# Instance norm on one core: 32 units of 4 MB in six slots, or 23 units of 4 and 6 MB in four slots

## The chip, the core and the metric

The kernel runs on one core of a Trainium2 chip. TensorE (PE in the profile), VectorE (DVE), ScalarE (ACT), GpSimd (POOL) and SyncE (SP) each follow their own instruction stream; 16 DMA engines move data between HBM, the chip's main memory, and SBUF, the on-chip memory of 128 partitions. The metric is the device time of one execution in microseconds (us), lower is better.

## The reference

```python
x: (4, 8, 16, 256, 256) float32          # 512 channels of 65536 places
gamma: (8, 16) float32                   # one factor for each of 128 channels
mu = x.mean(axis=(3, 4), keepdims=True)
var = ((x - mu) ** 2).mean(axis=(3, 4), keepdims=True)
out = (x - mu) / np.sqrt(var + 1e-5) * gamma[None, :, :, None, None]
```

Each channel is 256 KB. x is 134.2 MB and so is the output; x does not fit in SBUF, and every channel is read once and written once.

## The kernel before, in words

The flat array is cut into 32 units of 4 MB, 16 channels each. In SBUF a unit has 128 partitions with 8192 float32 (32 KB) in each, so that 8 partitions hold one channel. Six tiles `xt0` to `xt5` of 32 KB a partition are the slots; unit u lives in slot u % 6 (lines 45 to 48). Nothing is scheduled by a planner: each engine runs its instructions in the order in which the program writes them.

At the start, six loads are issued, units 1 and 3 on ACT's DMA queue and the others on SP's (lines 56 and 57). POOL issues two small transfers, a write of 16 times 512 B into the output (`touch`, line 54) and the read of gamma (line 55), and then makes `navg` (lines 63 to 72), a 128 x 128 matrix that holds -1/65536 wherever two partitions belong to one channel. DVE and PE spread gamma into `g_col`, one column for each of the eight possible positions of a unit (lines 80 to 91).

Then follows one loop over the units (line 104). For each unit:

- DVE sums each partition (line 106), ACT sums the squares (line 107);
- PE multiplies both sums with `navg` (line 115), which gives every partition minus its channel's mean and minus its mean square;
- DVE makes minus the variance (116), ACT its root (120), DVE the reciprocal (124) and the product with gamma (126);
- DVE normalises in place, (x - mu) * scale, one instruction over all 8192 columns (135). In unit 0 alone DVE takes 5120 columns and ACT the other 3072 (132);
- ACT's queue issues the store (139), and SP's queue issues the load of unit u + 6 (141). That load waits until the store of unit u has ended, since they share a slot.

Loads and stores thus stand in two queues, SP's and ACT's, which feed the same 16 DMA engines. Each transfer gives each engine eight rows, one row for each partition.

The program's lines follow.

Of the kernel before, what the change touches and what calls it, by code (L numbers as in the profile page):

```python
# [1 line left out]

# [4 lines left out]

F32 = mybir.dt.float32
U8 = mybir.dt.uint8
ALU = mybir.AluOpType  # L10
ACTF = mybir.ActivationFunctionType
AX = mybir.AxisListType


@with_exitstack
def kernel(
    ctx: ExitStack,
    tc: tile.TileContext,
    x: bass.AP,
    gamma: bass.AP,  # L20
    out: bass.AP,
):
    nc = tc.nc
    B, G, C, H, W = x.shape
    P = nc.NUM_PARTITIONS
    HW = H * W
    n_ch = B * G * C
    S = 8
    K = P // S
    F = HW // S  # L30
    U = n_ch // K
    NG = (G * C) // K
    AHEAD = 6
    assert HW % S == 0 and (G * C) % K == 0

    xv = x.rearrange("b g c h w -> (b g c h w)").rearrange("(u p f) -> u p f", p=P, f=F)
    ov = out.rearrange("b g c h w -> (b g c h w)").rearrange("(u p f) -> u p f", p=P, f=F)
# [9 lines left out]
    def load(u, queue):  # L47
        queue.dma_start(out=slots[u % AHEAD][:], in_=xv[u])  # L48


    g_row = singles.tile([1, G * C], F32, name="g_row")
    touch = singles.tile([16, 128], F32, name="touch")
    nc.vector.memset(touch[:], 0.0)  # L53
    nc.gpsimd.dma_start(out=ov[0][0::S, 0:128], in_=touch[:])  # L54
# [6 lines left out]
    one = singles.tile([1, 1], F32, name="one")  # L61
    nc.gpsimd.memset(one[:], 1.0)
    navg = singles.tile([P, K, S], F32, name="navg")
    nc.gpsimd.memset(navg[:], -1.0 / HW)  # L64
    nc.gpsimd.affine_select(  # L65
        out=navg[:], in_=navg[:], pattern=[[-S, K], [0, S]], compare_op=ALU.is_ge,
        fill=0.0, base=0, channel_multiplier=1,
    )
    nc.gpsimd.affine_select(  # L69
        out=navg[:], in_=navg[:], pattern=[[S, K], [0, S]], compare_op=ALU.is_ge,  # L70
        fill=0.0, base=S - 1, channel_multiplier=-1,
    )
    navg_w = navg[:].rearrange("p k s -> p (k s)")
    root_eps = singles.tile([P, 1], F32, name="root_eps")
    nc.scalar.activation(out=root_eps[:], in_=eps_t[:], func=ACTF.Sqrt)  # L75
    g_rep = singles.tile([1, NG, K, S], F32, name="g_rep")
    g_ps = psum.tile([P, NG], F32, name="g_ps", bufs=1)
    g_col = singles.tile([P, NG], F32, name="g_col")

    nc.vector.tensor_copy(  # L80
        out=g_rep[:],
        in_=g_row[:].rearrange("o (n k) -> o n k", n=NG).unsqueeze(3).to_broadcast([1, NG, K, S]),
    )
    for n in range(NG):
        nc.tensor.matmul(  # L85
            out=g_ps[:, n : n + 1],
            lhsT=g_rep[:, n].rearrange("o k s -> o (k s)"),
            rhs=one[:],
            start=True, stop=True,
        )  # L90
    nc.vector.tensor_copy(out=g_col[:], in_=g_ps[:])  # L91

    junk = singles.tile([P, F], U8, name="junk")

    st = singles.tile([P, U, 2], F32, name="st")
# [5 lines left out]
    shift = singles.tile([P, 1], F32, name="shift")  # L101

    squares = []
    for u in range(U):
        t = slots[u % AHEAD]
        nc.vector.reduce_sum(out=st[:, u, 0:1], in_=t[:], axis=AX.X)  # L106
        square = nc.scalar.activation(  # L107
            out=junk[:], in_=t[:], func=ACTF.Square, accum_out=st[:, u, 1:2],
        )
        if u:  # L110

            tc.declare_no_dep(square.ins, squares[-1].ins, reason="junk, ordered by the root between")
        squares.append(square)
        ps = psum.tile([P, 2], F32, name="ps")
        nc.tensor.matmul(out=ps[:], lhsT=navg_w, rhs=st[:, u], start=True, stop=True)  # L115
        nc.vector.tensor_scalar(  # L116
            out=nvar[:, u : u + 1], in0=ps[:, 0:1], scalar1=ps[:, 0:1],
            scalar2=ps[:, 1:2], op0=ALU.mult, op1=ALU.add,
        )
        nc.scalar.activation(  # L120
            out=std[:, u : u + 1], in_=nvar[:, u : u + 1], func=ACTF.Sqrt,
            bias=eps_t[:], scale=-1.0,
        )
        nc.vector.reciprocal(out=rstd[:, u : u + 1], in_=std[:, u : u + 1])  # L124
        g = u % NG
        nc.vector.tensor_mul(  # L126
            out=scale[:, u : u + 1], in0=rstd[:, u : u + 1], in1=g_col[:, g : g + 1],
        )
        cut = F * 5 // 8 if u == 0 else F
        if cut < F:  # L130
            nc.vector.tensor_mul(out=shift[:], in0=ps[:, 0:1], in1=scale[:, u : u + 1])  # L131
            nc.scalar.activation(  # L132
                out=t[:, cut:], in_=t[:, cut:], func=ACTF.Identity, bias=shift[:], scale=scale[:, u : u + 1],
            )
        nc.vector.tensor_scalar(  # L135
            out=t[:, :cut], in0=t[:, :cut], scalar1=ps[:, 0:1], scalar2=scale[:, u : u + 1],
            op0=ALU.add, op1=ALU.mult,
        )
# [6 lines left out]
_INS = ['x', 'gamma']  # L145
_OUTS = [((4, 8, 16, 256, 256), 'float32')]


# [23 lines left out]
```

## Time and profile before

| | |
|---|---|
| three runs | 626.85, 626.98, 627.24 us; median 626.98 |
| profiled execution | span 625.2 us; the profile has no other time for it, and the median lies 1.7 us above the span |
| bytes moved | 268.46 MB, a mean of 429 GB/s over the span |
| busy share of the span | DVE 71%, ACT 39%, PE 3%, POOL 0% |
| DMA engines | 9 tenths or more of every 40th of the span but the first and last, which show 8 |
| rows of 32 KB on the two queues | 4352 on ACT's (q10: 32 stores and 2 loads), 3840 on SP's (q1: 30 loads) |
| first unit landed, last unit landed | 22.8 us, 585.5 us |
| last store issued | 600.6 us |

In the profile, an engine's busy time counts only its computing instructions. DMA queues are numbered; q1 is the one that SP feeds and q10 the one that ACT feeds, q0 is POOL's. A transfer of the kernel appears in them as 128 data packets and 16 packets of 4 B, one for each DMA engine, which report its end. The profile's line numbers are those of the program above.

### The profile page before, as it was taken

How to read it: one execution, taken by the hardware profiler on the slowest of the kernel's cores; microseconds unless marked ns; L12 is line 12 of the kernel's file. 1: busy time of each engine (PE TensorE's matmuls, PEld its weight loads, DVE VectorE, ACT ScalarE, POOL GpSimd, SP SyncE). 2: the span in 40 equal slices, each digit the busy share in tenths (PEclk: the TensorE clock that was granted, in tenths of full speed). 3: DMA queues.
4: the chain of work that ended last, by engine and by line, in shares of the span. 5: the costliest groups of instructions: out<-in, count | busy, mean ns of one | idle time of the engine just before them, and what ended most of it. 6: DMA issues, size and time to landing. Idle time of an engine off the chain costs nothing.

```text
span 625.2 us, 635 instructions
## 1 busy us (share of the span) xinstructions
PE 21.4 (3%) x80; PEld 19.5 (3%) x80; DVE 441.8 (71%) x164; ACT 241.8 (39%) x99; POOL 2.4 (0%) x11
## 2 busy tenths in 40 slices
PE   0200000000000000000000000000000000000000
PEld 0200000000000000000000000000000000000000
DVE  0589999998776687666786767867668676687730
ACT  0464444444443244432344423444224442244400
POOL 1000000000000000000000000000000000000000
DMA  8999999999999999999999999999999999999998
GB/s 370 436 407 432 436 436 436 436 436 430 423 436 434 434 428 434 434 436 436 436 436 428 426 436 436 432 430 434 434 436 436 436 436 421 432 436 434 434 430 367
DMA packets 9282, 268.46 MB, mean 429 GB/s; under 512 B 1072, under 2 KB 1088, under 8 KB 1088
## 3 DMA queue, kind: packets, MB, share of 16 engines
q10 hardware_dynamic: 4896, 142.61, 52.9%
q1 hardware_dynamic: 4320, 125.83, 46.8%
q0 software_dynamic: 64, 0.01, 0.0%
q14 instruction: 2, 0.02, 0.0%
HBM read 134.22 MB, written 134.23 MB: 429 GB/s over the span
## 4 chain that ended last, share of the span: by engine, by line
another core or an unknown queue 61%; DMA 17%; DVE 15%; SPq 1%; PE 1%; issue 0%; ACT 0%
DMA xt<-in_x_dram 10%; DVE st L106 10%; DMA out_dram<-xt 8%; DVE xt L135 5%; SPq L48 1%; PE ps L115 1%; ACT std L120 0%; DVE nvar L116 0%; DVE rstd L124 0%; DVE scale L126 0%; DVE shift L131 0%
## 5 line engine op out<-in xcount | busy, mean ns | idle before, releaser
L106 DVE TENSOR_REDUCE st<-xt 128x1 f32<-128x8192 f32 x32 | 277.9, 8684 | 102.2 <-DMA xt<-in_x_dram 102.2
L107 ACT ACTIVATE junk<-xt 128x8192 uint8<-128x8192 f32 x32 | 225.0, 7030 | 272.0 <-DMA xt<-in_x_dram 233.8
L135 DVE TENSOR_SCALAR xt<-xt,ps,scale 128x8192 f32<-128x8192 f32 (+1 forms) x32 | 144.0, 4500 | 1.1
L120 ACT ACTIVATE std<-nvar,eps_t 128x1 f32<-128x1 f32 x32 | 9.4, 295 | 79.4 <-DVE nvar L116 79.4
L115 PE MATMUL ps<-st,navg 128*128 128x2 f32 x64 | 17.8, 348 | 557.3 <-DVE st L106 557.3
L115 PEld LDWEIGHTS ps<-st,navg 128*128 128x128 f32 x64 | 16.0, 310 | 559.1 <-issue 546.2
L116 DVE TENSOR_SCALAR nvar<-ps 128x1 f32<-128x1 f32 x32 | 9.2, 286 | 23.8 <-PE ps L115 23.8
L124 DVE RECIPROCAL rstd<-std 128x1 f32<-128x1 f32 x32 | 5.2, 163 | 11.6 <-ACT std L120 11.6
L80 DVE COPY g_rep<-g_row 1x1024 f32<-1x1024 f32 x1 | 0.7, 681 | 14.4 <-DMA g_row<-in_gamma_dram 14.4
L107 ACT ACTIVATION_READ_ACCUMULATOR junk<-xt 128x1 f32 x32 | 6.0, 186 | 0.0
L126 DVE TENSOR_TENSOR scale<-rstd,g_col 128x1 f32<-128x1 f32 x32 | 5.1, 158 | 1.1
L85 PE MATMUL g_ps<-one,g_rep 1*128 1x1 f32 x16 | 3.5, 347 | 16.3 <-DVE g_rep L80 16.3
L85 PEld LDWEIGHTS g_ps<-one,g_rep 1*128 1x128 f32 x16 | 3.5, 326 | 16.3 <-issue 16.3
L132 ACT ACTIVATE xt<-xt,shift,scale 128x3072 f32<-128x3072 f32 x1 | 2.9, 2947 | 0.7 <-DVE shift L131 0.7
L91 DVE COPY g_col<-g_ps 128x8 f32<-128x8 f32 x1 | 0.2, 167 | 3.7 <-PE g_ps L85 3.7
L75 ACT ACT_TABLE_LOAD x1 | 1.3, 1283 | 1.7 <-PEq L156 1.7
L53 DVE MEMSET touch<- 16x128 f32 x1 | 0.2, 165 | 0.9 <-PEq L156 0.9
L54 POOL DMA_DIRECT2D out_dram<-touch x1 | 0.6, 617 | 0.8 <-DVE touch L53 0.8
L55 POOL DMA_DIRECT2D g_row<-in_gamma_dram x1 | 0.5, 487 | 0.0
L65 POOL TENSOR_SCALAR_AFFINE_SELECT navg<-navg 128x128 f32<-128x128 f32 x1 | 0.4, 400 | 0.1
L69 POOL TENSOR_SCALAR_AFFINE_SELECT navg<-navg 128x128 f32<-128x128 f32 x1 | 0.4, 399 | 0.1
L64 POOL MEMSET navg<- 128x128 f32 x1 | 0.2, 230 | 0.0
(8 smaller groups left out, 1.0 us busy)
## 6 DMA issues: line engine op xcount, KB each, us to landing
out_dram<-xt ACTq DMA_DIRECT2D x32, 4096.0 KB, 62.5
xt<-in_x_dram SPq DMA_DIRECT2D x30, 4096.0 KB, 38.5
xt<-in_x_dram ACTq DMA_DIRECT2D x2, 4096.0 KB, 31.7
out_dram<-touch POOLq DMA_DIRECT2D x1, 8.0 KB, 9.3
g_row<-in_gamma_dram POOLq DMA_DIRECT2D x1, 0.5 KB, 13.5
```

Source lines behind the costliest of these rows:

```text
L48: queue.dma_start(out=slots[u % AHEAD][:], in_=xv[u])
L75: nc.scalar.activation(out=root_eps[:], in_=eps_t[:], func=ACTF.Sqrt)
L85: nc.tensor.matmul(out=g_ps[:, n : n + 1], lhsT=g_rep[:, n].rearrange("o k s -> o (k s)"), rhs=one[:], start=True, stop=True,)
L106: nc.vector.reduce_sum(out=st[:, u, 0:1], in_=t[:], axis=AX.X)
L107: square = nc.scalar.activation(out=junk[:], in_=t[:], func=ACTF.Square, accum_out=st[:, u, 1:2],)
L115: nc.tensor.matmul(out=ps[:], lhsT=navg_w, rhs=st[:, u], start=True, stop=True)
L116: nc.vector.tensor_scalar(out=nvar[:, u : u + 1], in0=ps[:, 0:1], scalar1=ps[:, 0:1], scalar2=ps[:, 1:2], op0=ALU.mult, op1=ALU.add,)
L120: nc.scalar.activation(out=std[:, u : u + 1], in_=nvar[:, u : u + 1], func=ACTF.Sqrt, bias=eps_t[:], scale=-1.0,)
L124: nc.vector.reciprocal(out=rstd[:, u : u + 1], in_=std[:, u : u + 1])
L126: nc.vector.tensor_mul(out=scale[:, u : u + 1], in0=rstd[:, u : u + 1], in1=g_col[:, g : g + 1],)
L132: nc.scalar.activation(out=t[:, cut:], in_=t[:, cut:], func=ACTF.Identity, bias=shift[:], scale=scale[:, u : u + 1],)
L135: nc.vector.tensor_scalar(out=t[:, :cut], in0=t[:, :cut], scalar1=ps[:, 0:1], scalar2=scale[:, u : u + 1], op0=ALU.add, op1=ALU.mult,)
```

## The change

Units now have 4 or 6 MB: two of 4, thirteen of 6, two of 4, five of 6 and one of 4, 23 in all. There are four slots of 48 KB a partition (the SBUF that the slots take stays at 192 KB a partition). A row of a 6 MB unit is 48 KB in a partition, which is three thirds of 4096 columns. A channel is 16 such thirds, so it starts in the first, second or third third of a partition, and a unit has 24 channels.

All loads are issued on SP's queue. The last unit is split between DVE and ACT in the normalising step as unit 0 is.

For a 6 MB unit the sums are made for each third (one DVE instruction with three results, three ACT instructions). Three PE products add them up into means on 72 partitions, where partition j * 24 + k stands for channel k as seen from third j (`navg3`). The variance, root, reciprocal and gamma are computed on these 72; `coef` puts minus the mean and the scale into column j of each; a fourth product with `back` brings them to the 128 partitions, one column a third (`wide`, in PSUM). DVE then normalises third by third, three instructions. Units of 4 MB go the old way. New helper matrices are made on POOL and DVE ahead of the loop, and gamma is spread in another way.

The core of the diff:

```diff
-    S = 8
-    K = P // S
-    F = HW // S
-    AHEAD = 6
+    F = 4096
+    SLOTS = 4
+    K = 24
+    sizes = [2] * 2 + [3] * 13 + [2] * 2 + [3] * 5 + [2]
+    U = len(sizes)
+    starts = [sum(sizes[:i]) for i in range(U)]
+    helped = (0, U - 1)
+    def rows(flat, u):
+        lo = starts[u] * P * F
+        return flat[lo : lo + sizes[u] * P * F].rearrange("(p f) -> p f", p=P)
-    psum = ctx.enter_context(tc.tile_pool(name="psum", bufs=4, space=bass.MemoryType.PSUM))
+    psum = ctx.enter_context(tc.tile_pool(name="psum", bufs=2, space=bass.MemoryType.PSUM))
-    slots = [data.tile([P, F], F32, name=f"xt{i}") for i in range(AHEAD)]
+    slots = [data.tile([P, 3 * F], F32, name=f"xt{i}") for i in range(SLOTS)]
+    def home(u):
+        return slots[u % SLOTS][:, : sizes[u] * F]
+    def load(u):
+        nc.sync.dma_start(out=home(u), in_=rows(xf, u))
-    for u in range(AHEAD):
-        load(u, nc.scalar if u in (1, 3) else nc.sync)
+    for u in range(SLOTS):
+        load(u)
...
+    navg2 = band("navg2", [P, 16, 8], -1.0 / HW, 0, 1, [[-8, 16], [0, 8]], 7)
+    in16 = band("in16", [P, 16], 1.0, 0, 1, [[-8, 16]], 7)
+    navg3 = band("navg3", [P, 3, 3, K], -1.0 / HW, 0, 3, [[1, 3], [0, 3], [-16, K]], 15)
+    mine = band("mine", [3 * K, 3], 1.0, 0, 1, [[-K, 3]], K - 1)
+    place = singles.tile([3 * K, 3, P], F32, name="place")
...
+    nc.vector.reduce_sum(out=back[:], in_=place[:].rearrange("q j p -> q p j"), axis=AX.X)
...
     for u in range(U):
+        t = home(u)
+        three = sizes[u] == 3
+        n = sizes[u] if three else 1
+        step = sizes[u] * F // n
+        nc.vector.reduce_sum(
+            out=st[:, u, :n, 0], in_=t.rearrange("p (j f) -> p j f", j=n), axis=AX.X,
+        )
+        for j in range(n):
+            square = nc.scalar.activation(
+                out=junk[:, :step], in_=t[:, j * step : (j + 1) * step],
+                func=ACTF.Square, accum_out=st[:, u, j, 1:2],
+            )
...
+        for j in range(n):
+            nc.tensor.matmul(
+                out=ps[:q],
+                lhsT=navg3[:, j].rearrange("p j k -> p (j k)") if three else navg2[:].rearrange("p k s -> p (k s)"),
+                rhs=st[:, u, j], start=j == 0, stop=j == n - 1,
+            )
...
+        if three:
+            nc.vector.tensor_scalar_mul(out=coef[:, u, 0], in0=mine[:], scalar1=ps[:q, 0:1])
...
+            nc.vector.tensor_scalar(
+                out=coef[:, u, 1], in0=mine[:], scalar1=rstd[:q, u : u + 1],
+                scalar2=g_ch[:, m : m + 1], op0=ALU.mult, op1=ALU.mult,
+            )
+            wide = psum.tile([P, 2, 3], F32, name="wide")
+            nc.tensor.matmul(
+                out=wide[:].rearrange("p v j -> p (v j)"), lhsT=back[:],
+                rhs=coef[:, u].rearrange("p v j -> p (v j)"), start=True, stop=True,
+            )
+            for j in range(3):
+                nc.vector.tensor_scalar(
+                    out=t[:, j * F : (j + 1) * F], in0=t[:, j * F : (j + 1) * F],
+                    scalar1=wide[:, 0, j : j + 1], scalar2=wide[:, 1, j : j + 1],
+                    op0=ALU.add, op1=ALU.mult,
+                )
...
-        nc.scalar.dma_start(out=ov[u], in_=t[:])
-        if u + AHEAD < U:
-            load(u + AHEAD, nc.sync)
+        nc.scalar.dma_start(out=rows(of, u), in_=t)
+        if u + SLOTS < U:
+            load(u + SLOTS)
```

More of the change, by code (lines that the diff above doesn't have):

```diff
@@ L43 @@
     ctx.enter_context(tc.manual_schedule())
-    slots = [data.tile([P, F], F32, name=f"xt{i}") for i in range(AHEAD)]
-    def load(u, queue):
-        queue.dma_start(out=slots[u % AHEAD][:], in_=xv[u])
-    g_row = singles.tile([1, G * C], F32, name="g_row")
+    slots = [data.tile([P, 3 * F], F32, name=f"xt{i}") for i in range(SLOTS)]
[3 more added lines that the diff above has]
+        nc.sync.dma_start(out=home(u), in_=rows(xf, u))
+    g_row = singles.tile([1, GC], F32, name="g_row")
@@ L62, with band @@
-    nc.gpsimd.memset(one[:], 1.0)
-    navg = singles.tile([P, K, S], F32, name="navg")
-    nc.gpsimd.memset(navg[:], -1.0 / HW)
-    nc.gpsimd.affine_select(
-        out=navg[:], in_=navg[:], pattern=[[-S, K], [0, S]], compare_op=ALU.is_ge,
+    ones = singles.tile([1, P], F32, name="ones")
+    nc.gpsimd.memset(ones[:], 1.0)
+    def band(name, shape, value, base, multiplier, pattern, top):
+        w = singles.tile(shape, F32, name=name)
+        nc.gpsimd.memset(w[:], value)
+        nc.gpsimd.affine_select(
+            out=w[:], in_=w[:], pattern=pattern, compare_op=ALU.is_ge,
+            fill=0.0, base=base, channel_multiplier=multiplier,
+        )
+        nc.gpsimd.affine_select(
+            out=w[:], in_=w[:], pattern=[[-a, n] for a, n in pattern], compare_op=ALU.is_ge,
+            fill=0.0, base=top - base, channel_multiplier=-multiplier,
+        )
+        return w
@@ new lines @@
+    nc.gpsimd.affine_select(
+        out=place[:], in_=place[:], pattern=[[-385, 3], [-3, P]], compare_op=ALU.is_ge,
+        fill=0.0, base=15, channel_multiplier=16,
+    )
+    root_eps = singles.tile([P, 1], F32, name="root_eps")
+    nc.scalar.activation(out=root_eps[:], in_=eps_t[:], func=ACTF.Sqrt)
+    nc.vector.reduce_sum(out=back[:], in_=place[:].rearrange("q j p -> q p j"), axis=AX.X)
+    eighth = singles.tile([3 * K, 9, 8], F32, name="eighth")
+    nc.gpsimd.memset(eighth[:], 1.0)
@@ L76 @@
[L76 to L89, printed above, removed]
-        )
@@ new lines @@
+    sixteens = sorted({8 * starts[u] % GC for u in range(U) if sizes[u] == 2})
+    g_some = singles.tile([P, 16], F32, name="g_some")
+    g_col = singles.tile([P, len(sixteens)], F32, name="g_col")
+    for n, c in enumerate(sixteens):
+        nc.vector.tensor_mul(out=g_some[:], in0=g_all[:, c : c + 16], in1=in16[:])
+        nc.vector.reduce_sum(out=g_col[:, n : n + 1], in_=g_some[:], axis=AX.X)
+    junk = singles.tile([P, 2 * F], U8, name="junk")
+    st = singles.tile([P, U, 3, 2], F32, name="st")
@@ L99 @@
     scale = singles.tile([P, U], F32, name="scale")
-    shift = singles.tile([P, 1], F32, name="shift")
+    shift = singles.tile([P, U], F32, name="shift")
+    coef = singles.tile([3 * K, U, 2, 3], F32, name="coef")
     squares = []
     for u in range(U):
[L105 to L108, printed above, removed]
-        )
-        if u:
-            tc.declare_no_dep(square.ins, squares[-1].ins, reason="junk, ordered by the root between")
-        squares.append(square)
-        ps = psum.tile([P, 2], F32, name="ps")
-        nc.tensor.matmul(out=ps[:], lhsT=navg_w, rhs=st[:, u], start=True, stop=True)
+        t = home(u)
[4 more added lines that the diff above has]
+            out=st[:, u, :n, 0], in_=t.rearrange("p (j f) -> p j f", j=n), axis=AX.X,
+        )
+        for j in range(n):
[3 more added lines that the diff above has]
+            )
+            if squares and j == 0:
+                tc.declare_no_dep(square.ins, squares[-1].ins, reason="junk, ordered by the root between")
+            squares.append(square)
+        q = 3 * K if three else P
+        ps = psum.tile([P, 2], F32, name="ps")
+        for j in range(n):
[4 more added lines that the diff above has]
+            )
```

100 lines of the change are left out of this document (65 added, 35 removed).

## The prediction

> **What bounds the kernel now.** I read the DMA part of the page first, since the page's chain of waits names mostly transfers, then cut the span into stretches, then looked at what the engines wait for.
>
> The queues, from the page (packets, MB, share of the 16 engines' time in the span):
>
> ```profile
> q10 hardware_dynamic: 4896, 142.61, 52.9%
> q1 hardware_dynamic: 4320, 125.83, 46.8%
> ```
>
> The two queues together take 99.7% of the DMA engines' time. The stretches say the same (columns: length, busy time of PE, PE's weight loads, DVE, ACT and POOL, the granted clock, DMA share, GB/s); the four are the loads alone, the first store's start, the long middle, and a part of the tail in which only stores are left:
>
> ```profile
> 2.00:31.00 29.00, 3.54 (x16) 3.48 (x16) 9.07 (x3) 8.34 (x4) 1.55 (x6) 1.00 0.99 425
> 31.00:47.00 16.00, 1.11 (x4) 1.00 (x4) 13.65 (x11) 10.66 (x5) 0.00 (x0) 1.00 0.99 406
> 47.00:585.00 538.00, 16.15 (x58) 14.50 (x58) 405.02 (x146) 215.10 (x87) 0.00 (x0) 1.00 1.00 433
> 600.00:620.00 20.00, 0.00 (x0) 0.00 (x0) 0.58 (x1) 0.00 (x0) 0.00 (x0) 1.00 1.02 439
> ```
>
> The DMA share is 1.00 for 538 us. In the trace's packet records nearly every 32 KB row takes 1213 ns and starts 1209 ns after the one before it on its DMA engine, for loads and stores, in the first slices of the middle as in the last, with both queues alive as with one. 16 x 32768 B / 1209 ns is 433.7 GB/s, the middle's 433. So the DMA engines bound the kernel, from their first packet at 1.8 us to their last at 623.9 us. SP's waits and the groups show the other side:
>
> ```profile
> SPq L48 <- DMA out_dram<-xt: 514.7, 26, 39.7
> ```
>
> ```profile
> L106 DVE TENSOR_REDUCE st<-xt 128x1 f32<-128x8192 f32 x32 | 277.9, 8684 | 102.2 <-DMA xt<-in_x_dram 102.2
> L107 ACT ACTIVATE junk<-xt 128x8192 uint8<-128x8192 f32 x32 | 225.0, 7030 | 272.0 <-DMA xt<-in_x_dram 233.8
> L135 DVE TENSOR_SCALAR xt<-xt,ps,scale 128x8192 f32<-128x8192 f32 (+1 forms) x32 | 144.0, 4500 | 1.1
> ```
>
> Loads wait 514.7 us for slots, and DVE, the busiest engine, still waits 102.2 us for loads. Neither wait costs anything as long as a row of some transfer stands ready for every DMA engine. The change is therefore worth what it does to the DMA engines' work, less any moment in which it leaves both queues empty.
>
> **The DMA work.** Each transfer gives each engine eight rows and one packet of 4 B.
>
> - Before: 64 transfers, 512 rows of 32 KB an engine: 512 x 1.209 = 619.0 us; 64 packets of 4 B, 6 ns each from start to start: 0.4. Sum 619.4.
> - A 48 KB row is not in the trace. The records have 512 B rows 23.3 ns from start to start, so the slope up to 32 KB is (1209 - 23.3) / (32768 - 512) = 0.03676 ns a byte and a row's fixed part is 23.3 - 18.8 = 4.5 ns. A 48 KB row is then 1209 + 16384 x 0.03676 = 1811.3 ns. From both sides: without any saving 1.5 x 1209 = 1813.5; cut into three pieces of 16 KB, 3 x (4.5 + 602.3) = 1820.3. I take 1811.3, since 1213 ns holds for 8192 rows without a sign of a further limit.
> - After: 46 transfers. The 5 units of 4 MB give 80 rows an engine, 96.7 us; the 18 of 6 MB give 288 rows, 521.65; 46 x 6 ns is 0.3. Sum 618.65.
>
> Difference: **-0.74 us**. The ends: the first packet starts at 1.8 us, and the 1.3 us behind the last packet stay. The remaining 2.7 us between first and last packet are start-up losses: the engines start up to 1.0 us apart, the first row takes 0.4 to 0.75 us more, and around 41.5 us, as the first store starts, each engine loses 0.3 to 1.2 us (mean about 0.85; it makes the 406 GB/s above). I keep them: after starts one load and one first store too. Bounds: the store's loss gone, -0.85; twice, +0.85.
>
> **Does a queue always have work?** What one 6 MB unit takes, from the rows:
>
> - Sum of a partition, L106: 8684 ns for 8192 columns, so 13.0 us for 12288.
> - Squares on ACT run beside it. L132's 3072 columns take 2.95 us and 8192 take 7.03, so 4096 take 3.8; three, with three reads of the sum at 0.19, 11.9 us. Hidden under 13.0; otherwise the excess would be added.
> - From the end of L106 to the start of L135 the trace has 1.8 us. Two more products (0.56 each), the fourth with its hand-over (0.75) and one more small DVE step (0.2) make 3.8.
> - Normalising: 5120 columns take 2.94, 8192 take 4.55, so 4096 take 2.4; three, 7.2. Both scalars now come from PSUM; before, one did, so I leave the price; bounds are 2.4 and, at L106's rate of 1.06 ns a column, 4.3 each.
>
> DVE needs 24.0 us a unit (29.7 at the worst bound). The DMA engines need 2 x 8 x 1.811 = 29.0. Round a slot: load 29.0 beside a store at equal shares, DVE 24.0, store 29.0, and about 4 for issue, first packet and report twice; 86 of 4 x 29.0 = 116 us. 30 us of the turn are waiting in queues.
>
> I followed the rows of one DMA engine through both queues, alternating while both have work. The same walk on the kernel before gives the last landing at 581 and the last row at 621.4, against 585.5 and 623.9 measured; the start-up losses make up the latter. After:
>
> - Start: the first loads alone fill SP's queue until 1.8 + 0.7 + 16 x 1.209 + 16 x 1.811 = 50.8 us. Unit 0 lands at 13, not at 22.8. DVE first finishes the new set-up. POOL's matrices have some 820 columns against 128 (each pass 0.23 to 0.40 us for 128): until about 10 us; gamma at 15.5 at the latest, as before; then some twenty small DVE steps of 0.16 to 0.4. Unit 0 starts between 14 and 20, and its store is issued at 28 to 34. Cover: 17 us; every us past that costs one.
> - Middle: the load of unit u + 4 is issued about 12 us before the load ahead of it ends, and a unit is ready about 20 us before its store's turn.
> - Tail: the last unit lands about 35 us before the end. It needs 8.7 + 1.8 + 3.0 + 1.6 = 15 us to its store, and ahead of it are 24 us of other stores. Unit 21 is ready 10 us before its turn. Cover 9 us.
>
> So nothing shows. The moved loads: units 1 and 3 leave ACT's queue for SP's; ACT saves two issues (0.4 us each), which bound nothing, and SP issues them in 0.33 each while the first rows run. The semaphore waits in the changed program's order name, for every load, the store of its slot and transfers that ended long before; no instruction waits ahead of a shorter one.
>
> Sum against the profiled execution: 625.2 - 0.74 = 624.5; with the 1.75 us by which the median lies above the span, **626.2 us**. That is -0.12%, inside the 0.2% (1.25 us) that a measurement of this kernel can tell from no change.
>
> **The rivals.**
>
> - *The store's start loses nothing* because no loads stand ahead of it in ACT's queue: 626.2 - 0.85 = 625.4. For it: in before the loss falls where ACT's queue goes from loads to stores. Against: it strikes SP's row at 41.5 hardest, which is a load.
> - *A fixed cost a transfer on a lone queue.* Hidden while the other queue has rows, bare where one is alone. After has two such boundaries at the start (SP alone until 30 us). Nearest row: 0.85 for a queue that starts; 2 x 0.85 = +1.7, 627.9. Against: the stores alone run at 439 GB/s across two boundaries. The Trainium skill's page "DMA: Bandwidth & Descriptors", section "Anatomy of one DMA — SWDGE (gpsimd) path", fits a transfer as 2.0 us plus bytes at 436 GB/s; exposed everywhere, that would make 18 fewer transfers worth 36 us, an estimate that the 433 GB/s of the middle refute, and at two boundaries alone 4 us.
> - *Rows are not moved whole.* In 16 KB pieces: 288 x 9.0 ns = +2.6, 628.8, slower. For it: no row above 32 KB is in the trace.
> - *DVE becomes the bound*: slower. It decides at 29.0 us of DVE a 6 MB unit; at 30.3 the 18 units wait 18 x 1.3 = 23 us, about 650. For it: the PSUM bound reaches 29.7, so 0.7 x 18 = 13, about 639. Against: L135 reads ps from PSUM already and keeps its rate.
>
> **How the numbers follow.** Forecast 0.49 (own range 625.8 to 627.0), store's start 0.25, lone queue 0.06, pieces 0.10, DVE 0.07, unnamed and slower 0.03. Faster by over 0.2% is the second, 0.25, with 0.01 from the forecast's edge; slower are pieces, DVE and the rest, 0.20; the rest 0.54. The range takes in all but DVE and the unnamed: 625.2 to 628.9.
>
> **What would show it.** Each of q1 and q10 with 23 x 144 = 3312 packets (pieces: above 7500); the stretch from 60 to 580 us at share 1.00 and 434 GB/s; rows of 48 KB at about 1815 ns; first store near 30 us with a dip of GB/s beside it; DVE near 24 us a unit and waiting for loads in every one. Wrong: a slice under 9 tenths in the middle or ahead of the last store, or DVE not waiting.

## The result, and the profile after

| | before | after |
|---|---|---|
| median | 626.94 us (626.78 to 627.28, 8 runs) | 628.17 us (627.15 to 629.76, 8 runs) |
| profiled execution | span 625.2 us | 627.41 us, span 625.7 us |

The ratio is 1.0022, 95% interval 1.0012 to 1.0032: slower by 1.2 us, where 0.7 us less was forecast. The runs of after also lie 2.6 us apart, those of before 0.5. (Ratios leave out single executions far above the others of their kernel, so for kernels whose runs scatter the ratio is smaller than that of the medians.) The profiled run of after, 627.41 us, is the second shortest of its eight.

The queues and the instruction fetches, from the page of after (packets, MB, share):

```profile
q1 hardware_dynamic: 3312, 134.22, 49.9%
q10 hardware_dynamic: 3312, 134.22, 49.6%
q14 instruction: 4, 0.03, 0.0%
q8 instruction: 1, 0.02, 0.0%
```

3312 is 23 x 144 for each queue: every 48 KB row is one packet. The records give it 1815 ns, and 1812 from start to start, where 1811.3 was forecast. The last two lines are engines that load their own instructions, by one packet for each block, called a fetch here; in before q14 has two packets. The prediction did not look at these lines.

Stretches of after, in the columns that the prediction names (`...` stands for lines not shown):

```profile
31.00:47.00 16.00, 0.56 (x2) 0.50 (x2) 14.82 (x6) 8.70 (x4) 0.00 (x0) 1.00 1.00 407
...
66.00:585.00 519.00, 25.26 (x140) 23.02 (x140) 378.43 (x145) 209.00 (x125) 0.00 (x0) 1.00 1.00 434
...
600.00:620.00 20.00, 0.56 (x2) 0.50 (x2) 3.66 (x6) 3.24 (x2) 0.00 (x0) 1.00 0.99 427
620.00:622.00 2.00, 0.00 (x0) 0.00 (x0) 0.00 (x0) 0.00 (x0) 0.00 (x0) 1.00 1.02 442
622.00:624.00 2.00, 0.00 (x0) 0.00 (x0) 0.00 (x0) 0.00 (x0) 0.00 (x0) 1.00 0.27 115
```

The same end in before:

```profile
620.00:622.00 2.00, 0.00 (x0) 0.00 (x0) 0.00 (x0) 0.00 (x0) 0.00 (x0) 1.00 0.83 360
622.00:624.00 2.00, 0.00 (x0) 0.00 (x0) 0.00 (x0) 0.00 (x0) 0.00 (x0) 1.00 0.42 180
```

The middle is as forecast, 434 GB/s at share 1.00. The news is in the end, from 622 to 624 us. A share of 0.42 or 0.27 does not say whether all engines stop together or a few go on; the packet records, below, do. The waits of SP's queue and the groups:

```profile
SPq L61 <- DMA out_dram<-xt: 537.8, 19, 45.8
```

```profile
L173 DVE TENSOR_REDUCE st<-xt 128x3 f32<-128x12288 f32 (+1 forms) x23 | 276.6, 12025 | 104.8 <-DMA xt<-in_x_dram 104.8
L177 ACT ACTIVATE junk<-xt 128x4096 uint8<-128x4096 f32 (+1 forms) x59 | 230.4, 3906 | 282.7 <-DMA xt<-in_x_dram 267.0
L215 DVE TENSOR_SCALAR xt<-xt,wide 128x4096 f32<-128x4096 f32 x54 | 127.6, 2420 | 13.3 <-PE wide L210 13.3
```

DVE waits 104.8 us for loads and loads wait 537.8 us for slots: no engine became the bound.

**The last DMA engine decides.** Each transfer gives each of the 16 DMA engines eight rows, even to one that is 17.9 us behind the others (sp_late5, below). The 4 B packet with which each engine closes the last store tells when it was done. In the profiled executions (us; the run's own time beside it):

```
kernel        median engine   last three            run
before           623.4        623.5 623.5 623.9     (span 625.2)
after            622.7        623.8 624.1 624.2     627.41
after2           624.6        625.5 626.3 627.7     630.89
lean             622.3        623.1 623.3 627.7     630.89
pad              623.5        623.6 624.7 627.8     630.79
padsplit         623.3        623.5 625.5 625.5     628.55
join             623.2        623.6 623.7 624.0     627.12
sp               623.5        624.0 625.6 627.0     630.31
actloads         622.7        624.2 624.8 626.1     629.20
after_late4      622.5        626.3 626.8 627.2     630.31
after_late6      622.4        623.3 623.7 626.7     629.84
sp_late5         665.5        665.6 665.6 668.5     671.75
```

In every line that has the run's time, this is 3.0 to 3.3 us above its last engine's end. The median engine of after ends 0.8 us before that of before, 622.7 against 623.4, close to the forecast -0.74. The mean of the sixteen falls by 0.27 us only, from 623.33 to 623.06, and the last engine ends 0.24 us later; in after2, the same kernel again, it ends 3.8 us later. So the rows shrank as forecast, and what single engines lose ate it.

### The profile page after: what moved, and what is told of

Read it like the earlier page. It is cut to its first block, busy times and chain, and to the rows that moved or that the text cites. A ratio compares the mean times of both kernels' runs of the same rounds, so it can differ in the third digit from the quotient of the medians.

```text
span 625.7 us, 854 instructions
## 1 busy us (share of the span) xinstructions
PE 29.1 (5%) x156; PEld 26.3 (4%) x156; DVE 446.7 (71%) x193; ACT 250.1 (40%) x145; POOL 6.3 (1%) x25
## 3 DMA queue, kind: packets, MB, share of 16 engines
q1 hardware_dynamic: 3312, 134.22, 49.9%
q10 hardware_dynamic: 3312, 134.22, 49.6%
## 4 chain that ended last, share of the span: by engine, by line
DMA 41%; another core or an unknown queue 37%; DVE 16%; PE 1%; ACT 1%; issue 1%; SPq 0%; POOL 0%; ACTq 0%
DMA out_dram<-xt 22%; DMA xt<-in_x_dram 17%; DVE st L173 10%; DVE xt L215 3%; DMA g_row<-in_gamma_dram 1%; DVE xt L235 1%; PE ps L187 1%; ACT xt L231 0%; SPq L61 0%; ACT std L196 0%; PE wide L210 0%; DVE nvar L192 0%; DVE rstd L202 0%; DVE g_col L153 0%
## 5 line engine op out<-in xcount | busy, mean ns | idle before, releaser
L173 DVE TENSOR_REDUCE st<-xt 128x3 f32<-128x12288 f32 (+1 forms) x23 | 276.6, 12025 | 104.8 <-DMA xt<-in_x_dram 104.8
L177 ACT ACTIVATE junk<-xt 128x4096 uint8<-128x4096 f32 (+1 forms) x59 | 230.4, 3906 | 282.7 <-DMA xt<-in_x_dram 267.0
L215 DVE TENSOR_SCALAR xt<-xt,wide 128x4096 f32<-128x4096 f32 x54 | 127.6, 2420 | 13.3 <-PE wide L210 13.3
L187 PE MATMUL ps<-st,navg 128*72 128x2 f32 (+1 forms) x118 | 18.1, 265 | 537.5 <-DVE st L173 537.5
L187 PEld LDWEIGHTS ps<-st,navg 128*72 128x72 f32 (+1 forms) x118 | 16.8, 239 | 539.2 <-issue 526.3
L196 ACT ACTIVATE std<-nvar,eps_t 72x1 f32<-72x1 f32 (+1 forms) x23 | 6.8, 295 | 69.6 <-DVE nvar L192 69.6
L192 DVE TENSOR_SCALAR nvar<-ps 72x1 f32<-72x1 f32 (+1 forms) x23 | 6.5, 284 | 22.4 <-PE ps L187 22.4
L235 DVE TENSOR_SCALAR xt<-xt,ps,scale 128x8192 f32<-128x8192 f32 (+1 forms) x5 | 19.5, 3908 | 0.1
L210 PE MATMUL wide<-coef,back 72*128 72x6 f32 x36 | 10.3, 357 | 23.2 <-DVE coef L205 23.2
L210 PEld LDWEIGHTS wide<-coef,back 72*128 72x128 f32 x36 | 9.0, 311 | 24.4 <-issue 19.1
```

The costliest lines, as they stand in the source:

```text
L173: nc.vector.reduce_sum(out=st[:, u, :n, 0], in_=t.rearrange("p (j f) -> p j f", j=n), axis=AX.X,)
L177: square = nc.scalar.activation(out=junk[:, :step], in_=t[:, j * step : (j + 1) * step], func=ACTF.Square, accum_out=st[:, u, j, 1:2],)
L187: nc.tensor.matmul(out=ps[:q], lhsT=navg3[:, j].rearrange("p j k -> p (j k)") if three else navg2[:].rearrange("p k s -> p (k s)"), rhs=st ...
L192: nc.vector.tensor_scalar(out=nvar[:q, u : u + 1], in0=ps[:q, 0:1], scalar1=ps[:q, 0:1], scalar2=ps[:q, 1:2], op0=ALU.mult, op1=ALU.add,)
L196: nc.scalar.activation(out=std[:q, u : u + 1], in_=nvar[:q, u : u + 1], func=ACTF.Sqrt, bias=eps_t[:q], scale=-1.0,)
L210: nc.tensor.matmul(out=wide[:].rearrange("p v j -> p (v j)"), lhsT=back[:], rhs=coef[:, u].rearrange("p v j -> p (v j)"), start=True, stop ...
```

## The experiments

Five theories of what holds single engines up. A, instruction fetches: after's profile has 854 instructions against 635, and a fetch may hold up a DMA engine that is at work on rows. B, rows of 48 KB. C, the loads moved to SP's queue, and with them the start. D, engines out of step: at the first store some engines take it one row later than others and then lose more in each transfer. E, loads and stores that do not end together. D and E came up while the experiments ran.

### Fewer instructions: lean

```diff
# after
-        n = sizes[u] if three else 1
+        n = 1
-        q = 3 * K if three else P
+        q = P
-        if three:
-            ... coef, wide, three products by thirds
+        if True:   # the way of the 4 MB units, over all columns
```

(In the diffs `...` stands for lines not shown.) It has the transfers of after and one instruction a step; it leaves out the sums by thirds, the squares of the last third and the means on 72 partitions.

> The changed kernel with its units, slots, queues and 48 KB rows, but with one instruction a step for the 6 MB units too: one sum over 12288 columns, one Square over 8192 of them, one product with navg2, one scale, one normalising instruction. It leaves out the sums by third, the last third's squares, the means on 72 partitions and their way back, so the values of 6 MB units are not the reference's. DVE falls from 193 to about 140 instructions, ACT by about 70, PE by about 110. Theory A (instruction fetches: the program's 8 KB blocks come over the same 16 DMA engines, each holds up one or two of them by 0.3 to 1.4 us, and the last engine sets the end): two or three fetches in the middle instead of five, 626.0 to 626.5 with a scatter under 0.7 us. Theory B (the 48 KB rows themselves stall or scatter): still 627.5 to 628.5 with a scatter of 2 us. Theory C (start with SP's queue alone): 627 to 628, engines' first rows and the first store as in the changed kernel.

Measured: 627.12 us (626.82 to 632.24, 12 runs) beside 627.33 of before on the same chip, ratio 1.0013 (0.9997 to 1.0028). Eight of the twelve lie from 626.82 to 627.32, about 1 us under after's median; the others reach 632.24. The profile has two fetches in mid-run instead of five packets. It caught a long run, 630.89, and shows it in the tail:

```profile
620.00:622.00 2.00, 0.00 (x0) 0.00 (x0) 0.00 (x0) 0.00 (x0) 0.00 (x0) 1.00 0.80 344
622.00:624.00 2.00, 0.00 (x0) 0.00 (x0) 0.00 (x0) 0.00 (x0) 0.00 (x0) 1.00 0.08 33
624.00:626.00 2.00, 0.00 (x0) 0.00 (x0) 0.00 (x0) 0.00 (x0) 0.00 (x0) 1.00 0.08 33
626.00:628.00 2.00, 0.00 (x0) 0.00 (x0) 0.00 (x0) 0.00 (x0) 0.00 (x0) 1.00 0.04 16
```

A share of 0.08 is 1.3 of 16 engines: for four microseconds the kernel waits for one. That engine fell behind in small steps from 138 to 589 us, 5.4 us in all, in both queues alike. The short runs speak for A, but lean alone does not show it: the intervals of lean and after overlap, and lean also differs from after in that all its engines take the first store after the same row (counted below).

### More instructions: pad, padsplit, afterpad

```diff
# pad: before             afterpad: after, the same with one [1, 16] tile
+        for i in range(16):
+            nc.vector.memset(pad[:, u, i : i + 1], 0.0)
# padsplit: before
+        for i in range(16):
+            (nc.vector if i % 2 else nc.gpsimd).memset(pad2[i % 2][:, u, i // 2 : i // 2 + 1], 0.0)
```

One element is written each time. DVE's writes stand where it waits for loads anyway; GpSimd's depend on nothing, and in padsplit all 256 have run before 16 us.

> The kernel before with 16 idle DVE writes of one element a unit behind the normalising step, 512 more instructions, about 1 us of DVE a unit out of the 4.4 us in which it waits for loads. Theory A: about four more fetches in the middle; the last DMA engine ends 0.5 to 1.5 us later, 627.5 to 628.5, and the scatter grows over the 0.5 us of before. Theories B and C: 626.9 as before.

> The kernel before with the same 512 idle one-element writes, half of them on GpSimd and half on VectorE. Theory A in the form that each engine's instruction blocks always come over the same DMA engine and their delays of 0.6 to 0.9 us add up there: two more fetches on VectorE's DMA engine instead of four, GpSimd's on another one, so 627.2 + 1.8 = 629.0 or a little less. If only the number of fetches counts: 630.4 again. If DVE's time counts: about 627.2 plus half of the 3.1 us too, but without steps at the fetches in the ends of one DMA engine.

> The changed kernel with 16 idle one-element DVE writes a unit, 368 more instructions: three more blocks of 128 for VectorE. Theory A, by the 0.8 us a fetch that the same writes cost in the kernel before: +2.4 to 2.7 us, 630.3 to 630.8, the scatter of the changed kernel on top. If the changed kernel's loss has nothing to do with fetches: 628 plus less than 1.

Measured: pad 630.39 us (630.36 to 630.79), 1.0054 (1.0042 to 1.0066); padsplit 628.55 (628.43 to 628.77), 1.0023 (1.0014 to 1.0032); afterpad 630.49 (629.65 to 631.31), 1.0057 (1.0043 to 1.0071). The fetches and the stretches of pad:

```profile
q14 instruction: 6, 0.05, 0.0%
```

```profile
585.00:620.00 35.00, 0.56 (x2) 0.50 (x2) 14.39 (x38) 7.42 (x3) 0.00 (x0) 1.00 1.01 434
620.00:624.00 4.00, 0.00 (x0) 0.00 (x0) 0.00 (x0) 0.00 (x0) 0.00 (x0) 1.00 0.65 279
624.00:628.00 4.00, 0.00 (x0) 0.00 (x0) 0.00 (x0) 0.00 (x0) 0.00 (x0) 1.00 0.06 25
```

0.06 is one engine. Its lag behind the median of the 16, read at the end of each transfer, is a staircase: +0.3 us, 1.0 after 57 us, 1.6 after 147, 2.5 after 272, 3.4 after 389, 4.3 after 506, and level between. Those times are five of pad's six fetches. The records do not name a fetch's engine; the sixth, at 199.5, stands at 199.4 in before, whose DVE has fewer instructions, so it is taken as ACT's and the five as DVE's. Padsplit also has six fetches in mid-run, but its late engines are two. One is 3.1 us behind by 42 us, after the fetches at 10.0 and 15.4, which are put down to GpSimd, and 2.2 from 217 us on; the other climbs to 2.2 by three steps, after 80.8, 234.1 and 428.6. Both end at 625.5, and it costs half of pad's loss, 1.5 us. So in pad a fetch of 8 KB costs one DMA engine 0.6 to 0.9 us, the same one each time, and the kernel pays the sum on the worst. That is A, shown for pad. It is one fetch for each 128 instructions of an engine (512 more bring four more). Afterpad, as expected, repeats it with 6 MB units: its latest engine falls back by 0.9 us at each of the fetches of 171, 320 and 480 us and ends at 627.0. In after, DVE has 205 instead of 170 instructions in the records, those of its queue counted too; by the same reading DVE and ACT fetch twice instead of once, and a fetch of 16 KB, taken as TensorE's, comes at 404 us.

### The loads' queue: sp, sp2, actloads, leanact, join

```diff
# sp, and sp2 on another chip: before
-        load(u, nc.scalar if u in (1, 3) else nc.sync)
+        load(u, nc.sync)
# actloads: after; leanact: lean
-        load(u)
+        load(u, nc.scalar if u in (1, 3) else nc.sync)
# join: before
-        load(u, nc.scalar if u in (1, 3) else nc.sync)
+        load(u, nc.scalar if u == 1 else nc.sync)
```

> The kernel before with the loads of units 1 and 3 on SP's queue too. Theory C: the first rows and the first store lose 0.3 to 0.6 us more a DMA engine, 627.2 to 627.6. Theories A and B: 626.9 as before, within 0.2.

> The changed kernel with the loads of units 1 and 3 on ACT's queue as before. Theory C: back to about 627.3 to 627.7. Theories A and B: 628.2 as the changed kernel, with its scatter of 2 us.

> The one-instruction-a-step version of the changed kernel (its 6 MB units' values are not the reference's, as before: thirds, the last third's squares and the 72-partition means are left out), with the loads of units 1 and 3 on ACT's queue. Theory A alone: as without the moved loads, 626.8 to 627.3 with now and then 628 to 632. Theory D (engines out of step since the first store finds SP's queue alone): the far runs disappear, all within 626.5 to 627.3. Theory B (48 KB rows): 627.5 to 628.5.

> The kernel before with all loads on SP's queue once more, on another day's chip: whether its scatter (627 to 648) belongs to the kernel or to that chip. Theory E: again a scatter of several us, since the first store finds SP's queue alone and two engines took it up one row later than the rest. If it was the chip: 627.0 to 627.6.

> The kernel before with only the load of unit 1 on ACT's queue; unit 3's goes to SP's. The first 20 us are as before, but ACT's queue then runs dry, and the first store at about 37 us finds SP's queue alone, as it does in the changed kernel and with all loads on SP's queue. Six slots, 32 KB rows, two fetches. Theory D (a queue that starts beside a lone one is taken up one row later by some DMA engines; these stay out of step, with loads ahead and stores behind, and lose about 0.1 us more at each transfer): 629 to 632 with a scatter of 1 to 3 us, and in the trace some engines 1.2 us or more behind in their stores and ahead in their loads from the first store on. If what matters is the start of the kernel on one queue: 627.0 with the scatter of before.

| | us, median (range, runs) | ratio (95%) |
|---|---|---|
| sp | 631.56 (627.12 to 648.18, 10) | 1.0045 (1.0024 to 1.0067) |
| sp2 | 630.74 (629.61 to 631.83, 5) | 1.0061 (1.0048 to 1.0074) |
| join | 627.12 (626.91 to 627.99, 11) | 1.0003 (0.9994 to 1.0012) |
| actloads | 629.20 (628.76 to 631.71, 6) | 1.0043 (1.0028 to 1.0059) |
| leanact | 627.92 (626.5 to 631.15, 12) | 1.0017 (1.0002 to 1.0031) |

The move alone costs before about 4 us: the prediction priced it at nothing. Sp's stretches:

```profile
47.00:585.00 538.00, 15.62 (x56) 14.03 (x56) 391.43 (x141) 211.73 (x86) 0.00 (x0) 1.00 1.00 433
...
620.00:624.00 4.00, 0.00 (x0) 0.00 (x0) 0.00 (x0) 0.00 (x0) 0.00 (x0) 1.00 0.68 295
624.00:627.00 3.00, 0.00 (x0) 0.00 (x0) 0.00 (x0) 0.00 (x0) 0.00 (x0) 1.00 0.08 33
```

The middle reads like before's, 433 GB/s; the loss is again one or two engines in the last 3 us. But C as such falls: the undoing in after (actloads) makes it slower, not faster. And join, whose first store also comes while SP's queue works alone, is as quick as before; D had expected 629 to 632 of it. Nor did leanact stay within the 626.5 to 627.3 that D gave it. What differs is seen by counting, for each DMA engine, the load rows from SP's queue that it moves before its first row of the first store:

```
before, pad, five      17 on all 16 engines
join                   23 on all 16
lean                   22 on all 16
actloads, leanact      16 on all 16
sp                     25 on 14,  26 on 2
sp2, sp_late2          25 on 12,  26 on 4
sp_late4               25 on 2,   26 on 13  (one not followed)
sp_late5               25 on 1,   26 on 15
after                  22 on 12,  23 on 4
after2, after_late2    22 on 10,  23 on 6
after_late4            22 on 3,   23 on 12,  24 on 1
after_late6            23 on 16
```

The two odd engines of sp stand at +1.5 and +1.7 us in the stores that end at 52 us, at +3.3 and +4.5 in those at 575, and end the kernel at 625.6 and 627.0. The engines change rows within about 0.9 us of one another; a store that starts within that time finds some before and some after the change. In before, join and pad, with 32 KB rows and all engines in step, lags but those of the fetches stay within 1.3 us. That is theory D. In after it fits less well: its four odd engines stand 2.2 to 2.3 us behind in the stores that end at 56 us and 2.2 to 2.7 in those at 371, so most of them hardly drift.

The odd engines stay odd. From 60 to 560 us the rows of 14 engines in sp alternate strictly, load and store, as all 16 do in before. The two others move, once in each transfer of 19.4 us, two rows of one queue one after another, and so meet every boundary at another moment than the 14. This is no price in itself: join has such a pair on all 16 engines in every transfer and pays nothing, and in sp_late5, below, 15 engines have it and the one that has not falls behind. What goes with the loss in these kernels is to differ.

### Shifting the first store: sp_late2, sp_late4, sp_late5, after_late2, after_late4, after_late6

```diff
# sp, or after; k = 2, 4, 5 or 6
+        if u == 0:
+            for _ in range(k):
+                nc.scalar.activation(out=root_eps[:], in_=eps_t[:], func=ACTF.Sqrt)
         nc.scalar.dma_start(out=ov[u], in_=t[:])
```

Each idle operation takes ACT 0.2 us. Not all of it reaches the store: in the profiles its issue moves from 28.80 us in sp to 28.91, 29.57 and 29.79, and from 29.00 in after to 29.11, 29.57 and 29.98.

> The kernel before with all loads on SP's queue, and two idle ACT operations (0.2 us each) ahead of the first store's issue. In the trace of that kernel the first store arrived while the DMA engines changed rows at 31.7 to 32.5 us; the two engines that changed first took one more load row. Theory D (an engine that is a row out of step, loads ahead and stores behind, loses more at each transfer, and so the scatter): 0.4 us later about half of the engines miss the store: 629 to 633 with a scatter of some us. If the step of a row doesn't matter: the same as without the delay by other means, 627 to 632, or 627.1 if the lone queue doesn't matter either.

> The same with four idle operations, 0.8 us. Theory D: now all engines have changed rows before the store arrives and take it after the same row; all in step, 627.0 to 627.4 with the scatter of before. If the step of a row doesn't matter: as with two.

> The changed kernel with its first store issued 0.4 us later. In its trace the first store came while four of the engines had just begun another load row; 0.4 us later more should miss it. Theory D: as the changed kernel or worse, 628 to 629, scatter 2 us or more.

> The changed kernel with its first store issued 0.8 us later; the engines' row changes lay within 0.7 us, so nearly all should take the store after the same row. Theory D: part of the loss goes, 627.2 to 627.6, with most runs within 0.5 us. If only the fetches cost: 627.9 to 628.2 as the changed kernel.

> The kernel before with all loads on SP's queue and five idle ACT operations of 0.2 us ahead of the first store's issue, one more than in sp_late4. Out of step: the DMA engines of sp change rows within about 0.9 us of one another, 1.21 us apart; with 1.0 us of delay nearly all of them should meet the first store one row later than in sp, all alike. Then nothing drifts: 627.0 to 627.4 us, lags of less than 1 us at the end. If one to three engines still stand apart from the rest, they drift by more than 2 us and it is 629 to 655. Rival, that a load queue that works alone until the first store comes costs the same whenever the store comes: 630 to 632 as in sp, without a relation to the delay.

> The kernel after with six idle ACT operations of 0.2 us ahead of the first store's issue. Out of step: the rows of the first 6 MB loads change 1.81 us apart; 1.2 us of delay should bring the engines that were one row late in after_late4 and the others back to one row. Then 627.2 to 627.6 us, the rest over the forecast being the two further instruction fetches of DVE at 0.4 to 0.9 us each. If some engines still stand apart, 628.5 to 630.5. Rival, that the delay itself is what made after_late4 slower: 630.8 to 631.3, in proportion to it.

| | us, median (range, runs) | ratio (95%) |
|---|---|---|
| sp_late2 | 635.38 (629.76 to 652.38, 7) | 1.0097 (1.0064 to 1.0129) |
| sp_late4 | 653.95 (644.17 to 674.15, 6) | 1.0300 (1.0284 to 1.0317) |
| sp_late5 | 672.91 (643.68 to 674.72, 6) | none: the runs lie too far apart |
| after_late2 | 628.74 (627.6 to 631.82, 12) | 1.0032 (1.0022 to 1.0042) |
| after_late4 | 630.50 (630.2 to 631.99, 5) | 1.0062 (1.0049 to 1.0075) |
| after_late6 | 629.62 (628.77 to 629.84, 5) | 1.0039 (1.0026 to 1.0052) |

The cure that I expected of sp_late4 and sp_late5 failed: delays of 0.8 and 1.0 us bring 13 and 15 engines over, and leave two and one behind. For that case D had given 629 to 655 us in sp_late5; four of its six runs are above. After_late4, too, has 12 engines alike and not all, and misses the 627.2 to 627.6 expected. The stretches of sp_late5:

```profile
47.00:585.00 538.00, 14.51 (x52) 13.02 (x52) 363.75 (x131) 196.74 (x79) 0.00 (x0) 1.00 1.00 420
585.00:620.00 35.00, 1.12 (x4) 1.00 (x4) 20.41 (x10) 7.99 (x6) 0.00 (x0) 1.00 0.79 335
620.00:640.00 20.00, 0.56 (x2) 0.50 (x2) 14.06 (x6) 7.63 (x4) 0.00 (x0) 1.00 0.52 224
640.00:668.00 28.00, 0.55 (x2) 0.50 (x2) 13.64 (x5) 7.20 (x3) 0.00 (x0) 1.00 0.59 255
```

The odd engine takes the store one row earlier than the others, so its loads come later: +1.3 us at 51 us, +6.5 at 90, +10.6 at 149, +17.9 at 307. Each load lands when this engine has its share, so units, stores and slots come later, and in the end the queues run dry (0.79, 0.52, 0.59 where before has 1.02 from 600 to 620 us). The runs of sp_late4 (644.17 to 674.15) and sp_late5 (643.68 to 674.72) cover the same range, so the 19 us between their medians mean little. But every one of them is 16 us or more above before, and neither a delay of 1.0 us nor a lone queue costs that by itself: after_late6 has the delay, join the lone queue.

After_late6 is the cleanest test in the 6 MB kernel: its store is issued 1.0 us later than after's, and all 16 engines take it alike. Its start and tail:

```profile
31.00:47.00 16.00, 0.59 (x2) 0.50 (x2) 14.63 (x6) 9.60 (x4) 0.00 (x0) 1.00 1.04 434
...
620.00:622.00 2.00, 0.00 (x0) 0.00 (x0) 0.00 (x0) 0.00 (x0) 0.00 (x0) 1.00 0.80 344
622.00:624.00 2.00, 0.00 (x0) 0.00 (x0) 0.00 (x0) 0.00 (x0) 0.00 (x0) 1.00 0.12 49
624.00:626.00 2.00, 0.00 (x0) 0.00 (x0) 0.00 (x0) 0.00 (x0) 0.00 (x0) 1.00 0.08 33
```

The dip of the first store reads 434 GB/s against 407, but is smaller rather than gone: by the packet records the rows of this stretch take 0.6 us an engine longer than their usual 1213 or 1815 ns, 1.0 in after. 12 engines end between 622.0 and 622.5, and it is quicker than after_late4, where four engines end at 626.2 to 627.2. But it does not reach the 627.2 to 627.6 that I expected, nor the rival's 630.8: one engine still falls back. It does so in steps of 0.1 to 2 us, several of them beside fetches (at 109, 402 and 558 us), others between, and ends at 626.7; and between 450 and 496 us four more fall out of step, by 1.8 to 3.1 us in their stores. With 629.62 us it is also slower than after itself, 628.17 and 627.92. So D is not shown to be what after loses: taking the store alike did not make it quicker.

### Slots and larger rows: five, rows64

```diff
# five: before
-    AHEAD = 6
+    AHEAD = 5
# rows64: units of 4 and 8 MB, three tiles of 64 KB a partition used as six halves
+    sizes = [1] * 4 + [2] * 13 + [1] * 2
+    ... sums and squares by halves, two averaging matrices, the last unit split too
+        load(u, nc.scalar if u in (1, 3) else nc.sync)
```

> The kernel before with five slots instead of six, all else as it was: rows of 32 KB, two instruction fetches, loads 1 and 3 on ACT's queue. With six slots a load waits in SP's queue behind the one that runs, and in the trace of before every load ends together with a store on all DMA engines; with five the next load is issued only when a store has ended, so that loads and stores get out of step by a row or more. Both queues should still never be empty together. Theory E (the scatter comes from transfers of the two queues that do not end together: an engine that is late then loses more at each transfer): a scatter of 1 to 5 us and a median of 627.5 to 630. Theory A alone, or B (long rows): 627.0 with the scatter of before, 0.8 us.

> Fewer and longer rows and fewer instructions at once: four units of 4 MB, thirteen of 8 MB with 64 KB rows (four partitions a channel, one instruction a step, two for the squares and two products), two of 4 MB; the three tiles are used as six halves, loads 1 and 3 on ACT's queue. Rows by the slope: 48... 16 x 6 rows of 32 KB and 16 x 13 of 64 KB an engine, 96 x 1.209 + 208 x 2.4135 = 618.1 against 619.0, less 26 packets of 4 B: 1.1 us less work; one fetch on VectorE and one on ScalarE as before. Theory A: 626.0 to 626.5 if the queues stay full; the tail has little cover here, which may cost up to 2 us. If a row of 64 KB is cut in two: 627.

Five: 628.93 us (628.57 to 629.51), 1.0033 (1.002 to 1.0045). That is the time that E gave, but not for E's reason: loads and stores no longer end together, and yet lags stay level after 87 us, so E falls. Its loss is in one stretch, where SP's queue runs dry and starts again:

```profile
62.00:80.00 18.00, 0.56 (x2) 0.50 (x2) 16.82 (x6) 7.42 (x3) 0.00 (x0) 1.00 1.00 395
80.00:585.00 505.00, 15.07 (x54) 13.54 (x54) 371.51 (x136) 200.42 (x81) 0.00 (x0) 1.00 1.00 433
```

Rows64: 631.45 us (630.45 to 634.99), 1.0078 (1.0058 to 1.0097), where A gave 626.0 to 626.5 and up to 2 us for the tail. Its 64 KB rows are whole packets too, and it has the fewest of all kernels here, yet:

```profile
83.00:92.00 9.00, 0.00 (x0) 0.00 (x0) 9.00 (x1) 8.97 (x3) 0.00 (x0) 1.00 1.06 390
92.00:552.00 460.00, 11.81 (x48) 11.13 (x48) 308.65 (x60) 163.88 (x58) 0.00 (x0) 1.00 1.00 434
552.00:565.00 13.00, 0.00 (x0) 0.00 (x0) 12.63 (x1) 12.60 (x3) 0.00 (x0) 1.00 0.97 411
```

The rate of the middle is 434, no better than with 48 KB. It loses at the changes between unit sizes (390 and 411 GB/s; in the first of the two stretches rows take 1.5 us an engine longer than usual), and three engines end 2.5 us or more after the rest, though all took the first store alike. This speaks for B, though no run isolates it: of the kernels with 48 or 64 KB rows whose engines took the first store alike, lean, actloads, after_late6 and rows64 have engines that fall back all the same in the profiled run, and in leanact two fell out of step later, between 62 and 81 us. In before, join and pad, with 32 KB rows, none but the engine of the fetches drifts by more than 1.3 us.

### After once more: after2

> The changed kernel unaltered, on the same chip as the other three. All theories: about 628, with a scatter of 2 us, which the engines' ends in the trace should show as a few engines that lose time after instruction fetches (theory A) or that are out of step with the others from the first store on (theory D: an engine that does not change rows together with the others loses some 0.1 us more at each transfer).

627.92 us (627.15 to 630.89, 12 runs), 1.0015 (1.0005 to 1.0025). Its profiled run is the longest of the twelve; its last engine ends at 627.7, and six engines were odd at the first store instead of four. The same program falls into step differently from run to run, which fits its scatter.

## Why the prediction was wrong

- **The DMA work: right.** Packets, whole rows and the rate came as worked out, and the median engine ends 0.8 us sooner for -0.74 forecast. Pieces, 0.10, did not come. None of the signs named as wrong showed either: they looked at the middle and at the engines, and the loss is in the last 2 us.
- **"Does a queue always have work?": right.** A 6 MB unit takes DVE 12.95 + 3 x 2.42 and a chain of 2.9, about 23 us for 24.0 forecast. Unit 0 landed at 13.2 us and its store was issued at 29.0 (28 to 34); the last store at 605.0. DVE as the bound did not come; PSUM scalars cost nothing (2420 ns for 2.4 us).
- **"I keep them": the step that failed.** The sum took the 2.7 us of losses between first and last packet as the same for all engines and both kernels. It worked with the mean engine, but the last one sets the end. On average an engine takes 621.26 us from its first row to its last packet in before and 621.00 in after: 0.26 less, where the rows give 0.74 less, so that each lost about 0.5 us more. And the last engine stands 1.1 us behind the mean in after, 0.6 in before. The two take back all of the 0.74 and 0.24 more, by which the last engine ends later. The bounds of the store's loss, 0.85 on either side, were thought of as a moment for every engine: the rows of that stretch lose 1.0 us an engine in after, 0.8 in before, but the first store of after also costs four engines a place in the order.
- **Added instructions at nothing: wrong.** They are hidden on their engines, as I said of each, but their fetches go through the resource that is the bound: pad and afterpad show it. How much of after's own loss they make is not measured. The Trainium skill's page "Runtime: NRT & Kernel Launch", section "Instruction fetch mechanics", calls the cost of crossing a block of instructions, 16 KiB there and 8 KB in these traces, "mostly hidden". Pad shows it hidden from the issuing engine and bare on a DMA engine, at 0.6 to 0.9 us each.
- **"The moved loads … bind nothing": not safe.** In before the same move costs about 4 us, and it changes at which row the engines stand as the first store comes. In after, moving two loads back gains nothing (actloads), so what the move costs there is not shown.
- **The store's start** was a rival at 0.25. Its dip stayed (407 GB/s for 406); after_late6 has a smaller one and is slower, so the time does not follow it.
- **The rival of a lone queue** gave 627.9, near the result, by luck: join has a lone queue and pays nothing. That 628.17 lies within the range of 625.2 to 628.9 is luck too, for none of its terms is what after lost.

How the 2.0 us between forecast and median divide is not settled. Lean's median is about 1 us below after's, but lean is in step besides, and leanact, with the same few instructions, has after2's 627.92. Fetches, engines out of step and drift with larger rows are the candidates, and after's runs differ from one another. Why an engine out of step loses 0.1 us a transfer in sp is open: in sp_late5 the extra time stands mostly in load rows (63 of 85 us, summed over the engines from 60 to 300 us), and no record names what they wait for. Why larger rows drift is open too. No version here beats before.

## What to carry to other kernels

Where the DMA engines are the bound, look at each of the 16, not at their mean: rows are dealt out evenly, so a stall of one cannot be made up by the others, and a gain below a microsecond can be smaller than one of them. Price added instructions by their fetches, one for each 128 on an engine, and look whether the fetches of an engine fall on one DMA engine. After a change of the start, count the rows that each DMA engine moved before the first store; every kernel here whose counts differ scatters by 1.7 us or more, though some with equal counts do too.

## What was not expected of the hardware

- An instruction fetch of 8 KB for 128 instructions costs a fully used DMA engine 0.6 to 0.9 us, the same DMA engine for all of DVE's in pad (five steps); two engines are late, by 2.2 us each, where DVE and GpSimd share the instructions (padsplit).
- One DMA engine of 16, one row out of order at the first store, goes with a time of 671.75 us in the profiled run (sp_late5; before 626.86 on the same chip).
- 64 KB rows reach 434 GB/s, as 48 KB rows do and 433 with 32 KB.
